# Nineteen adds from GpSimd to VectorE, and written-out tables of buffer places and of instruction orders on all five engines

## The chip, the cores and the metric

One core of a Trainium2 chip runs the kernel. The metric is the device time of one execution in microseconds, lower is better. A core has a matrix engine (TensorE, PE in the profile), three engines that work on tiles (VectorE, DVE; ScalarE, ACT; GpSimd, POOL), a sync engine that here only issues transfers (SyncE, SP), and 16 DMA engines. Each engine works through its own list of instructions in order, and an instruction that has to wait for a semaphore holds up those behind it on its engine.

## The reference

One decoder layer in fp32 with 512 tokens and a model width of 1024. Three token mixers read one normed input, each is gated, and their sum is projected back; a SwiGLU layer follows. Cut to the shape of it:

```python
u = rms_norm(h, ln_mix_pre)
qa, ka, va, qb, kb, vb, qm, gl = split(u @ w_in)
y_swa = sliding_window_attention(qa, ka, va, sinks, rel_bias)   # 8 heads, 2 kv heads, window 128
y_sb  = stick_breaking_attention(qb, kb, vb)                    # 8 heads
y_mem = softmax_attention(qm, rms_norm(mem, ln_mem) @ w_mem_kv) # 4 heads, 256 memory rows
g = sigmoid(gl)                                                 # 3 gates of (512, 1024)
merged = g0 * (y_swa @ w_branch_swa) + g1 * (y_sb @ w_branch_sb) + g2 * (y_mem @ w_branch_mem)
h = h + rms_norm(merged @ w_out, ln_mix_post)
u = rms_norm(h, ln_ffn_pre)
ffn = (silu(u @ w_gate) * (u @ w_up)) @ w_down                  # width 2816
return h + rms_norm(ffn, ln_ffn_post)
```

## The kernel before

**Products.** Each fp32 operand is split into a rounded part (`hi`, or a name that ends in `h`) by a copy on ScalarE (line 137) and the rest (`lo`, or `l`) by a subtraction on VectorE (line 138). A product is three matmuls, lines 169, 170 and 171. The three large products (the gates' part of `w_in`, gate and up, down) are done blockwise with seven products of half-size operands instead of eight, called `p1` to `p7`. Sums of weight blocks that these need are partly formed by the transfers: GpSimd issues a load that adds to a buffer which SyncE's load has filled (line 446 for the gates, 1224 for gate and up, 1364 and 1367 for down).

**Streams.** A `Stream` holds units in the order in which TensorE uses them: a weight tile is loaded some units ahead, split three units ahead, and its matmuls are issued. `dn` is the stream of the token mixers, `fs` that of gate and up. Between the units the program writes the attention work. From this written order, priorities and the dependences, a scheduler at build time makes the list of each engine; pins such as `after(ins, first)` add an order between two instructions without a wait.

**Buffers.** Weight tiles have rings of four (`raw`, `hi`, `lo`); 73 buffers of 128x512 (`ck`) rotate; in PSUM two banks (`psd`) and six (`psa`) rotate apart. For the second half the pools of weights and constants are closed and a new pool of nine raw buffers is opened (`fp`).

**Gates.** `g2p` is the PSUM tile of the third mixer's gate product and `g0p` that of the first's. When a product is complete, `q_end` takes it out: for `p1`, `p5`, `p6` and `p7` by a ScalarE copy (line 540, `gq2p`), which is also what frees the bank for the next product. A branch product `br` (`branch_t`) is multiplied by its gate on VectorE (line 599), and the sum with the other branches is one more add (line 602): GpSimd does it for 14 of the 16 tiles. `merge` transposes the sum, `wo` is the output projection's weight and `mx` its product; `mix` norms it into `mt` (lines 1111 to 1116), `turn` transposes `mt` into `ut`, and `place` (lines 1153 and 1154) writes its split blocks (`B11h` and `B11l` and so on) for the gate and up products `gx`, `gy` and `gw`.

**Down.** `dn_mm` makes the products `x`, `y` and `w` from tiles of `w_down` (`r`, 128x1024, and `bp`, 128x512) and the activations (`aq`, split to `lh` and `ll`). In `p7` the tiles `bp30` to `bp310` of `p3` are used a second time after an adding load.

```python
                g = gate_t[(b, t, h)]
                with tc.high_priority():
                    nc.vector.tensor_tensor(g[:, :], ps[:, :], g[:, :], op=ALU.mult)
                eng = nc.vector if (b, t) == (MEM, NT - 1) else nc.gpsimd
                more = acc_t[(t, h)] if b == SWA else gate_t[(SWA, t, h)]
                eng.tensor_tensor(g[:, :], g[:, :], more[:, :], op=ALU.add)
```

## Time and profile before

| | |
|---|---|
| time, three runs | 787.07, 787.52 and 788.17 us, median 787.52 |
| the profiled execution | 787.54 us, of which the span is 785.7 us |
| granted TensorE clock | 0.999 |
| busy: TensorE / VectorE / ScalarE / GpSimd | 776.3 / 595.4 / 469.3 / 123.2 us |
| the chain that ended last | 93% TensorE, 2% DMA, 2% VectorE, 1% ScalarE |
| moved by DMA | 128.61 MB, mean 164 GB/s |

The span runs from the first instruction to the last; 1.8 us of the profiled time lie around it. Busy is the time in which an engine has an instruction of its own in work. Matmuls are pipelined: a row's duration reaches into the next row, so how fast TensorE goes is read from the distance between two starts.

### The profile page before, as it was taken

To read this page: it belongs to the slowest core of one execution; us is meant where nothing else is said; L and a number is where in the kernel's file an instruction comes from. 1 tells how busy PE (TensorE), PEld (TensorE's weight loads), DVE (VectorE), ACT (ScalarE), POOL (GpSimd) and SP (SyncE) were. 2 spreads that over 40 slices of the span, in tenths; PEclk is the share of its full clock that TensorE was granted. 3 is DMA by queue.
4 is the path that set the end of the run, shared out by engine and by line. 5 is a ranking of instruction groups with operands and counts; after the bars stand their busy time and mean duration, and the time that the engine had idled before them with its cause. 6 is when DMAs were issued, how large, how long until landed. Compare 5 with 4: busy or idle time off the path is not lost.

```text
span 785.7 us, 12335 instructions
## 1 busy us (share of the span) xinstructions
PE 776.3 (99%) x4638; PEld 682.2 (87%) x4638; DVE 595.4 (76%) x942; ACT 469.3 (60%) x837; POOL 123.2 (16%) x142
## 2 busy tenths in 40 slices
PE   9999999999999999999999999999999999999996
PEld 6899887788888888887888899999999999888885
DVE  6995876686877757876855599867677777898797
ACT  7663676686577666657633577455554455666673
POOL 0203400002011111321261000100000000215200
PEclk9999999999999999999999999999999999999999
DMA  8444923265449794369849418987666651949802
GB/s 301 132 138 121 314 88 108 81 190 124 89 100 206 178 208 139 54 170 250 304 162 255 92 47 219 260 220 191 186 180 183 186 155 54 222 107 239 184 1 108
DMA packets 44220, 128.61 MB, mean 164 GB/s; under 512 B 5248, under 2 KB 6832, under 8 KB 44160
## 3 DMA queue, kind: packets, MB, share of 16 engines
q1 hardware_dynamic: 30480, 85.21, 32.8%
q0 software_dynamic: 13248, 42.22, 27.8%
q8 instruction: 36, 0.59, 0.3%
q10 hardware_dynamic: 432, 0.39, 0.1%
q14 instruction: 24, 0.20, 0.1%
HBM read 120.98 MB, written 4.72 MB: 160 GB/s over the span
## 4 chain that ended last, share of the span: by engine, by line
PE 93%; DMA 2%; DVE 2%; issue 1%; ACT 1%; POOL 0%; DVEq 0%; SPq 0%; ACTq 0%; POOLq 0%
PE gx L169 5%; PE gx L171 5%; PE gx L170 5%; PE gy L171 3%; PE gy L169 3%; PE gy L170 3%; PE x L171 3%; PE x L170 3%; PE x L169 3%; PE br L169 2%; PE br L170 2%; PE br L171 2%; PE mx L171 2%; PE mx L170 2%; PE mx L169 2%; PE g1p L169 2%
## 5 line engine op out<-in xcount | busy, mean ns | idle before, releaser
L137 ACT CAST hi<-gw 128x1024 fp32r<-128x1024 f32 x77 | 79.9, 1048 | 92.7 <-DVE gw L1242 39.6
L138 DVE TENSOR_TENSOR lo<-raw,hi 128x1024 fp32r<-128x1024 f32 (+2 forms) x82 | 99.9, 1219 | 46.2 <-ACT hi L137 45.7
L138 DVE TENSOR_TENSOR lo<-gw,hi 128x1024 fp32r<-128x1024 f32 x77 | 93.5, 1223 | 36.2 <-ACT hi L137 36.2
L137 ACT CAST hi<-raw 128x1024 fp32r<-128x1024 f32 (+2 forms) x82 | 85.2, 1042 | 43.4 <-PE pv L171 13.0
L1224 POOL DMA_DIRECT2D gw<-in_w_gu x27 | 23.3, 883 | 196.4 <-DMA gw<-in_w_gu 91.3
L870 DVE TENSOR_TENSOR_SCAN bw<-br,bw 128x512 f32<-128x512 f32 (+3 forms) x32 | 24.4, 808 | 17.0 <-ACT bw L194 17.0
L137 ACT CAST hi<-r 128x1024 fp32r<-128x1024 f32 (+1 forms) x24 | 23.6, 982 | 19.8 <-PE y L171 5.3
L446 POOL DMA_DIRECT2D raw<-in_w_g x24 | 20.7, 862 | 93.2 <-DVE lo L138 74.2
L170 PE MATMUL x<-lo,lh 128*128 128x512 f32 x88 | 34.2, 389 | 0.0
L169 PE MATMUL x<-hi,lh 128*128 128x512 f32 x88 | 34.2, 389 | 0.0
L171 PE MATMUL x<-hi,ll 128*128 128x512 f32 x88 | 34.1, 389 | 0.0
L138 DVE TENSOR_TENSOR lo<-r,hi 128x1024 fp32r<-128x1024 f32 (+1 forms) x24 | 27.1, 1130 | 3.7 <-ACT hi L137 3.6
L137 ACT CAST hi<-bp 128x512 fp32r<-128x512 f32 x33 | 19.3, 620 | 13.4 <-PE y L171 4.8
L138 DVE TENSOR_TENSOR lo<-bp,hi 128x512 fp32r<-128x512 f32 x33 | 22.7, 721 | 6.0 <-ACT hi L137 5.8
L169 PE MATMUL gx<-B11h,hi 128*128 128x256 f32 x88 | 25.1, 285 | 0.2 <-ACT B11h L1153 0.2
L169 PE MATMUL gx<-T4h,hi 128*128 128x256 f32 x88 | 25.0, 285 | 0.0
L169 PE MATMUL gy<-N22h,hi 128*128 128x256 f32 x88 | 25.0, 284 | 0.0
L171 PE MATMUL gy<-N22h,lo 128*128 128x256 f32 x88 | 25.0, 284 | 0.0
L171 PE MATMUL gw<-B21h,lo 128*128 128x256 f32 x88 | 25.0, 284 | 0.0
L170 PE MATMUL gx<-B11l,hi 128*128 128x256 f32 x88 | 25.0, 284 | 0.0
L170 PE MATMUL gw<-B21l,hi 128*128 128x256 f32 x88 | 24.9, 283 | 0.0
L169 PE MATMUL gy<-T1h,hi 128*128 128x256 f32 x88 | 24.9, 283 | 0.0
(824 smaller groups left out, 2758.7 us busy)
## 6 DMA issues: line engine op xcount, KB each, us to landing
gw<-in_w_gu SPq DMA_DIRECT2D x57, 512.0 KB, 4.8
gw<-in_w_gu POOLq DMA_DIRECT2D x27, 512.0 KB, 7.5
raw<-in_w_g POOLq DMA_DIRECT2D x24, 512.0 KB, 6.0
raw<-in_w_g SPq DMA_DIRECT2D x18, 512.0 KB, 3.9
raw<-in_w_p SPq DMA_DIRECT2D x14, 512.0 KB, 4.5
raw<-in_w_brt SPq DMA_DIRECT2D x12, 512.0 KB, 4.8
bp<-in_w_dn SPq DMA_DIRECT2D x22, 256.0 KB, 10.3
r<-in_w_dn POOLq DMA_DIRECT2D x10, 512.0 KB, 9.1
```

Of the source, the lines that this page charges most:

```text
L137: ins = nc.scalar.copy(hi, raw)
L138: lows = nc.vector.tensor_tensor(lo, raw, hi.bitcast(F32), op=ALU.subtract)
L169: one = nc.tensor.matmul(out, lh, rh, start=start, stop=False, skip_group_check=True)
L170: nc.tensor.matmul(out, lh, rl, start=False, stop=False, skip_group_check=True)
L171: return one, nc.tensor.matmul(out, ll, rh, start=False, stop=stop, skip_group_check=True)
L446: nc.gpsimd.dma_start(t[:, :], src, accum_op=ALU.add)
L870: st["scan"] = nc.vector.tensor_tensor_scan(x, r, x, 0.0, op0=ALU.mult, op1=ALU.add)
L1224: nc.gpsimd.dma_start(gw[(n, key)][:, :], g_src(n, i, j), accum_op=ALU.add)
```

## The change

Nineteen tile operations leave GpSimd for VectorE: the 14 gate adds of line 602, three adds of the memory's squares (line 390), one add of 128x256 in `rstd_of` (line 232) and one subtraction of 32x128 (line 810). Six scalings of broadcast gains by -0.5 (line 1058) leave GpSimd for ScalarE. The arithmetic is the same.

Two sets of tables are written out. `PLAN` gives every tile its buffer: four places each for `raw`, `hi` and `lo`, eight PSUM banks `p0` to `p7` that both pools now share, 73 `ck` places, 16 small ones; one pool of weights and constants (`wide0`) stays open through both halves. `ORDER` gives, for each of the five engines, the whole list of its instructions by the number in which the program issues them; `follow` chains each to the one before it, and the pins of `after` fall away. The tables were drawn up with longer transfer times. Smaller edits: the copies `ur` of `turn` are issued later (`kept`), two loads of gate and up move from unit 4 to unit 5, and some tiles are taken when first used (`Late`).

```diff
+ORDER = {
+    "tensor": (
+        "0-17 19 18 20-709 716 719 710-715 717-718 720-754 761 764 755-760 762-763 765-927 940-943 933-936 944 "
...
+    "gpsimd": (
+        "5-12 4 2-3 16 0 29 1 14 13 15 30 17 22 27 21 20 19 18 23 28 25 24 26 31-34 36-37 35 38 40 39 41-49 51 50 "
+        "52-65 70 66 69 71 67-68 72-95 107-112 96-99 103 101 100 102 104-106"
+    ),
...
+PLAN = {
+    "raw": (
+        "0 3 2 1 0 3 2 1 0 3 2 1 0 3 2 1 0 3 2 1 0 3 2 1 0 3 2 1 0 3 2 1 0 3 2 1 0 3 2 3 2 3 2 1 0 1 0 1 0 3 1 2 0 "
...
-    nc = tc.nc
+    nc = Core(tc.nc)
+    places = Places()
...
-    psd = ctx.enter_context(tc.tile_pool(name="psd", bufs=2, space=bass.MemoryType.PSUM))
     psa = ctx.enter_context(tc.tile_pool(name="psa", bufs=6, space=bass.MemoryType.PSUM))
+    psd = psa if PLAN else ctx.enter_context(tc.tile_pool(name="psd", bufs=2, space=bass.MemoryType.PSUM))
...
     def after(ins, first):
+        if not ORDER:
+            follow(ins, first)
+
+    def follow(ins, first):
         dep = mybir.DependencyInfo(mybir.DependencyClass.NoSync, mybir.DependencyReason.DATA)
         tc.add_manual_dep(ins.ins, first.ins.name, dep, reason="order")
...
         if acc.shape[1] > n:
-            nc.gpsimd.tensor_tensor(acc[:, :n], acc[:, :n], acc[:, n : 2 * n], op=ALU.add)
+            nc.vector.tensor_tensor(acc[:, :n], acc[:, :n], acc[:, n : 2 * n], op=ALU.add)
...
             if acc is None:
                 acc = x
             else:
-                nc.gpsimd.tensor_tensor(acc[:, :], acc[:, :], x[:, :], op=ALU.add)
+                nc.vector.tensor_tensor(acc[:, :], acc[:, :], x[:, :], op=ALU.add)
...
-                eng = nc.vector if (b, t) == (MEM, NT - 1) else nc.gpsimd
+                eng = nc.vector
...
-            nc.gpsimd.tensor_scalar(t[h][:, :], t[h][:, :], -0.5, None, op0=ALU.mult)
+            nc.scalar.mul(t[h][:, :], t[h][:, :], -0.5)
...
             for h in range(2):
                 place(("B11", "B21")[h], t, pt[h])
-                nc.scalar.copy(turned[t][h][:, :], pt[h][:, :])
+            st[("kept", t)] = pt
             return
...
-    load_at(4, g_raw, 0, "t", 1, 0)
-    load_at(4, g_plus, 0, "t", 0, 0)
+    load_at(5, g_raw, 0, "t", 1, 0)
+    load_at(5, g_plus, 0, "t", 0, 0)
...
+    for e, text in ORDER.items():
+        seen, last = getattr(nc, e).seen, None
+        for part in text.split():
+            a, _, b = part.partition("-")
+            for k in range(int(a), int(b or a) + 1):
+                if last is not None:
+                    follow(seen[k], seen[last])
+                last = k
```

In the changed kernel every instruction carries line 185, the wrapper's, so its rows are told apart by engine, operation and tile: `p3` is PSUM bank 3, `hi1`, `lo1` and `raw2` are weight places.

ScalarE in the gate products of the third mixer, before. `gq2p50` and `gq2p51` are the copies that free the banks of product `p5`; `hi127` is the rounded part of a weight that an adding load completes:

```order
L194 ACTIVATE gq2p11_3618<-gq2p11_3618,rs_x_299 128x512
L137 CAST hi127_3695<-raw112_3191 128x1024
L540 COPY gq2p50_3706<-g2p50_3671 128x512
L540 COPY gq2p51_3718<-g2p51_3679 128x512
L137 CAST hi128_3720<-raw113_3193 128x1024
L137 CAST wo10h_3737<-wo10_3714 128x512
L137 CAST wo11h_3741<-wo11_3716 128x512
```

The same place after; `hi1_77<-raw2_74` in its last row is the weight of `hi127`:

```order
L185 ACTIVATE gq2p11_3164<-gq2p11_3164,wide0_84 128x512
L185 CAST wo10h_3267<-wo10_3246 128x512
L185 CAST wo11h_3271<-wo11_3248 128x512
L185 COPY gq2p50_3238<-p3_107 128x512
L185 CAST wo02h_3308<-wo02_3290 128x512
L185 COPY gq2p51_3250<-p0_104 128x512
L185 CAST hi1_77<-raw2_74 128x1024
```

The two copies have moved from behind the weight's cast to ahead of it, and three casts of `wo` tiles from behind the copies to ahead of them.

ScalarE some 15 us on, at the end of product `p7`, before; `wo12` and `wo13` are tiles of the output projection that SyncE loads:

```order
L194 ACTIVATE gq2p60_3800<-gq2p60_3800,rs_x_299 128x512
L137 CAST wo12h_3835<-wo12_3809 128x512
L194 ACTIVATE gq2p61_3813<-gq2p61_3813,rs_x_299 128x512
L137 CAST wo13h_3839<-wo13_3811 128x512
L137 CAST hi135_3846<-raw132_3816 128x1024
L540 COPY gq2p70_3856<-g2p10_3586 128x512
L540 COPY gq2p71_3869<-g2p11_3593 128x512
```

The same place after:

```order
L185 ACTIVATE gq2p60_3324<-gq2p60_3324,wide0_84 128x512
L185 ACTIVATE gq2p61_3337<-gq2p61_3337,wide0_84 128x512
L185 COPY gq2p70_3374<-p2_106 128x512
L185 CAST hi0_76<-raw0_72 128x1024
L185 COPY gq2p71_3387<-p4_108 128x512
L185 CAST hi3_79<-raw3_75 128x1024
L185 CAST hi2_78<-raw1_73 128x1024
L185 CAST wo12h_3356<-wo12_3333 128x512
```

The copies of `p7` now follow the two sigmoids at once; `wo12h`, `wo13h` and the cast of `hi135` (now `hi3_79`) stand behind the first of them or both.

TensorE where gate and up begin, before. `gx0` is the first product of gate and up, `gw0` a second one beside it, and `hi151` to `hi153` are the rounded weights of `gx0`, `gw0` and the next product, `gx1`:

```order
L171 MATMUL gx0_4612<-B11h0_3502,lo151_4384 128x256
L169 MATMUL gx0_4612<-B11h1_3504,hi151_4383 128x256
L169 MATMUL gw0_4660<-B21h0_3506,hi152_4493 128x256
L170 MATMUL gw0_4660<-B21l0_3507,hi152_4493 128x256
L170 MATMUL gx0_4612<-B11l1_3505,hi151_4383 128x256
L171 MATMUL gx0_4612<-B11h1_3504,lo151_4384 128x256
```

The same place after. `p2` is `gx0`, `p7` is `gw0`, `p6` is `ut21` (transposes of the normed rows `mt21`), and `p3` is `gx1`, in the bank that held one half of the projected rows (`mx30`) until then:

```order
L185 MATMUL p2_106<-B11h0_3918,lo0_80 128x256
L185 MATMUL p2_106<-B11h1_3922,hi1_77 128x256
L185 MATMUL p7_111<-B21h0_3926,hi3_79 128x256
L185 MATMUL p6_110<-c_ident_329,mt21_3887 128x128 x2
L185 MATMUL p3_107<-B11h0_3918,hi2_78 128x256
L185 MATMUL p3_107<-B11l0_3919,hi2_78 128x256
L185 MATMUL p3_107<-B11h0_3918,lo2_82 128x256
```

The second matmul of `gw0` and the rest of `gx0`'s first half have moved back, and seven matmuls of `gx1` and two transposes have come ahead of them. Just ahead of this piece, the first matmul of `gx0` stood behind the transposes of `ut10` and `ut11` and ahead of the four of `ut20`; it now stands behind three of those four as well.

GpSimd's adding loads of `bp30` to `bp310` in `p7` of down stood in the order 30, 31, 32, 33, 34, 35, 36, 37, 38, 39, 310 and stand now in the order 30, 31, 32, 33, 37, 35, 34, 36, 38, 39, 310. The two scalings of `bc_g_fpost` that stood among them are gone from GpSimd.

More of the change, by code (lines that the diff above doesn't have):

```diff
@@ L1 @@
 import math
[L2 removed]
+from contextlib import ExitStack, nullcontext
 import numpy as np
@@ L147, in w_load @@
         uid[0] += 1
-        raw = wp.tile([P, 1024], F32, tag="raw", name=f"raw{uid[0]}")
+        raw = places.take(wp, "raw", [P, 1024], F32, f"raw{uid[0]}")
         nc.sync.dma_start(raw[:, :n], src)
@@ L215, in tile_kernel @@
     nc.vector.memset(eps_t, EPS)
-    ones = cst.tile([P, P], F32, name="ones")
+    ones = places.fixed(cst, [P, P], F32, "ones")
     nc.vector.memset(ones[:, :], 1.0)
@@ L342, in val @@
         return gen
-    v_all = cst.tile([P, NT * 640], F32, name="v_all")
+    v_all = places.fixed(cst, [P, NT * 640], F32, "v_all")
     def own_values(t):
@@ L730, in first_split @@
         split(raws[i][:, sl], his[i][:, sl], los[i][:, sl])
-    with tc.manual_schedule():
-        idle = cst.tile([P, 512], BF16, name="idle")
+    with nullcontext() if ORDER else tc.manual_schedule():
+        idle = places.fixed(cst, [P, 512], BF16, "idle")
         nc.vector.memset(idle[:, :], 0.0)
@@ L1360, in dn_issue @@
             if p == "p1":
-                rr[c] = fp.tile([P, 1024], F32, tag="raw", name=f"r{c}")
+                rr[c] = places.take(fp, "fraw", [P, 1024], F32, f"r{c}")
                 nc.sync.dma_start(rr[c][:, :n], src)
```

155 lines of the change are left out of this document (125 added, 30 removed), and 91 rows, old and new, of tables (ORDER, PLAN).

## The prediction

> **What bounds the kernel now.** I read the page's busy times first, then the windows of 100 us, then the waits of TensorE, then the chain that ended last around those waits. The page:
>
> ```profile
> PE 776.3 (99%) x4638; PEld 682.2 (87%) x4638; DVE 595.4 (76%) x942; ACT 469.3 (60%) x837; POOL 123.2 (16%) x142
> ```
>
> The windows, with columns span, then busy time and count of TensorE, its weight loads, VectorE, ScalarE and GpSimd, the granted clock and the DMA share:
>
> ```profile
> 0.00:100.00 100.00, 98.64 (x505) 84.12 (x506) 78.74 (x121) 58.58 (x95) 23.11 (x38) 1.00 0.61 199
> ...
> 300.00:400.00 100.00, 98.56 (x480) 82.46 (x480) 71.77 (x102) 59.93 (x106) 25.54 (x22) 1.00 0.59 169
> 400.00:500.00 100.00, 99.83 (x649) 91.07 (x648) 75.93 (x140) 54.07 (x120) 17.59 (x17) 1.00 0.67 177
> 500.00:600.00 100.00, 100.00 (x836) 100.00 (x835) 75.41 (x89) 50.21 (x71) 9.46 (x11) 1.00 0.72 192
> ...
> 700.00:786.00 86.00, 79.29 (x350) 65.31 (x348) 70.86 (x121) 51.27 (x99) 17.71 (x19) 0.99 0.56 132
> ```
>
> TensorE is the bound nearly everywhere, at the full clock. The rows shown lack 1.36 us in the first window, 1.44 in the fourth, 0.17 in the fifth, and the end; they sum to 476.3 of the page's 776.3, so the three left out are full. The waits of TensorE name the same places (engine and line, what it waited for, total, times, longest):
>
> ```profile
> PE g2p L169 <- ACT gq2p L540: 1.4, 2, 1.0
> PE warm L181 <- DVE idle L735: 1.4, 1, 1.4
> PE gx L169 <- ACT B11h L1153: 0.2, 1, 0.2
> ```
>
> The end of TensorE, from the chain (start, duration, what):
>
> ```profile
> 779.07 0.24 PE x L171
> ```
>
> The last matmul is over at 779.31 and the span is 785.7, so 6.4 us follow TensorE: the last norm and the store. Neither this tail nor the start of the first matmuls is touched by the change, and the matmuls are the same in number and shape. What the change can win is therefore what TensorE idles in the middle, 1.6 us by these rows; what it can lose has no such bound.
>
> **The change part by part.** First the two waits for `gq2p`. TensorE around them (start, duration):
>
> ```profile
> 353.88 0.39 PE L171 MATMUL g2p<-hi,xsp51l 128*128 128x512 f32 x1
> 355.02 0.39 PE L170 MATMUL g2p<-lo,xsp51h 128*128 128x512 f32 x1
> 355.24 0.39 PE L171 MATMUL g2p<-hi,xsp51l 128*128 128x512 f32 x1
> 356.60 0.50 PE L169 MATMUL g2p<-hi,xsp30h 128*128 128x512 f32 x1 [0.97 <-ACT gq2p L540]
> 372.82 0.39 PE L171 MATMUL g2p<-hi,ul 128*128 128x512 f32 x1
> 373.68 0.50 PE L169 MATMUL g2p<-hi,uh 128*128 128x512 f32 x1 [0.47 <-ACT gq2p L540]
> ```
>
> Two starts are 0.22 to 0.23 us apart when nothing waits (355.02 to 355.24). At the first wait they are 1.36 us apart, so it costs 1.13; at the second 0.86, so it costs 0.63. Together 1.76 us, a little more than the idle time of the waits view, since the refill of the pipeline counts too. The chain says what held the copies up:
>
> ```profile
> 344.73 10.19 DMA raw<-in_w_g
> 355.01 0.67 ACT hi L137
> 355.97 0.59 ACT gq2p L540
> 365.13 5.29 DMA wo<-in_w_out
> 370.44 0.62 ACT wo12h L137
> 371.60 0.60 ACT wo13h L137
> 372.20 0.96 ACT hi L137
> 373.16 0.48 ACT gq2p L540
> ```
>
> The first copy stood on ScalarE behind a cast whose weight landed at 354.92, though its product was complete at 353.88 + 0.39 = 354.27. In the new order the copy stands ahead of that cast. It then runs from 354.3 to 354.9, and TensorE wants the bank at 355.24 + 0.23 = 355.47: 0.5 us to spare, and the wait is gone. The cast of the weight that was in front is late next; by the rows of the program its first matmul comes after 24 others of the product, some 5.4 us later, against 1.05 for the cast and about 1.2 for VectorE's part, so it stays covered. The second copy of the pair has a `wo` cast of 0.6 us ahead of it and must be done by about 356.8, six matmuls later; its product ends at 355.63, so it ends near 356.3. At the second place the copies now stand ahead of the casts of `wo12` and `wo13`, which waited for a load of 5.29 us. Even by the old times the sigmoids before them are over at 371.6, where `wo13h` began; the product is complete at about 371.85, the copy ends near 372.5, and TensorE wants it at 372.82 + 0.23 = 373.05. Gain: 1.13 + 0.63 = 1.76 us. Both hold as long as ScalarE is not late there by more than half a microsecond; without that cover up to 1.76 us come back.
>
> Next, where gate and up begin. TensorE, ScalarE and VectorE there:
>
> ```profile
> 449.04 1.04 PE L1165 MATMUL ut<-c_ident,mt 128*128 128x128 f32 x8
> 450.25 0.39 PE L169 MATMUL gx<-B11h,hi 128*128 128x256 f32 x1 [0.17 <-ACT B11h L1153]
> 450.53 0.22 ACT L194 ACTIVATE r_m<-t_m 128x1 f32<-128x1 f32 x1
> 451.03 0.21 DVE L1082 SCALAR_TENSOR_TENSOR t_m<-r_m,v_m 128x1 f32<-128x1 f32 x1
> 451.49 0.15 DVE L1083 SCALAR_TENSOR_TENSOR r_m<-t_m,r_m 128x1 f32<-128x1 f32 x1
> 451.89 1.40 DVE L1114 SCALAR_TENSOR_TENSOR mt<-mx,r_m,bc_g_post 128x512 f32<-128x512 f32 x2
> ```
>
> The wait for `B11h` was 0.17 to 0.33 us. Three transposes now stand ahead of it, which hides it. But `gx1` comes forward into the bank that `mt` still reads. Its place is near 451.75: 450.25, then one and seven matmuls of 0.12 (100 us for 836 of them, in the window from 500) and five transposes of 0.11. The `mt` that it waits for can start when `r_m` is there: ScalarE gives its part at 450.75, two small VectorE steps of 0.21 and 0.15 follow, and one `mt` takes half of 1.40, so it ends near 452.0. That is a new wait of 0.25 us for an old one of about 0.3. I count nothing here; the ends are -0.3 and +0.5.
>
> The adds. One GpSimd add, and VectorE beside it:
>
> ```profile
> L602 DVE TENSOR_TENSOR gq2p<-gq2p,gq0p x2: 681/739/797, 391.6 to 404.2; 128x512 f32<-128x512 f32 x2
> 383.06 1.29 POOL L602 TENSOR_TENSOR gq2p<-gq2p,gq0p 128x512 f32<-128x512 f32 x1 [22.22 <-DVE gq2p L599]
> 383.42 1.48 DVE L138 TENSOR_TENSOR wo14l<-wo,wo14h 128x512 fp32r<-128x512 f32 x1 [0.51 <-ACT wo14h L137]
> 384.83 0.68 DVE L138 TENSOR_TENSOR wo15l<-wo,wo15h 128x512 fp32r<-128x512 f32 x1
> ```
>
> On VectorE an add takes 0.74 us (the first row, a median in ns). Seventeen of 128x512 make 12.6 us and the two small ones at most 1. Against that, a VectorE operation that met a GpSimd add took 1.48 where its like took 0.68, so 0.8 us come back for each that meets one: nothing to 14 x 0.8 = 11 us. VectorE's sum grows by 2 to 13 us out of 785, and I take 4. The Trainium skill's "SBUF — State Buffer", section "Who interferes with whom", gives a reason: a VectorE instruction with two SBUF inputs contends with a GpSimd instruction that reads SBUF, and the loser blocks for the whole instruction. By it the second row's 1.29 us less the 0.36 that had passed would be lost, 0.93 against the 0.80 measured, and VectorE's sum would grow by nearly nothing; the trace agrees within 0.15 us. None of it lies on TensorE's path unless VectorE itself runs out of time. The six scalings cost ScalarE about 0.59 each (the `gq2p` copy's row), 3.5 us beside an engine that is 60% busy: nothing.
>
> The transfers. In `p7` of down, the second half of `w_down` tile `bp34` has gone from fifth to seventh of GpSimd's adding loads. ScalarE's casts of these tiles and TensorE's first use:
>
> ```profile
> 733.12 0.62 ACT L137 CAST hi<-bp 128x512 fp32r<-128x512 f32 x1 [1.61 <-PE y L171]
> 736.94 0.62 ACT L137 CAST hi<-bp 128x512 fp32r<-128x512 f32 x1 [1.42 <-PE x L170]
> 738.90 0.62 ACT L137 CAST hi<-bp 128x512 fp32r<-128x512 f32 x1 [1.34 <-DMA bp<-in_w_dn]
> 739.69 0.39 PE L169 MATMUL x<-hi,lh 128*128 128x512 f32 x1
> ```
>
> The tiles come 2 us apart (736.9, 738.9), the fifth at 733.1 and the seventh at 736.9, by the starts of their casts. With cast (0.62) and subtraction (0.68) `bp34` is ready at 738.2, and the matmul that needs its `lo` is the one behind 739.69. The cover shrinks from some 5.5 us to 1.7. I take nothing, with 0 to 3.3 us as the ends (the rival below prices it). The first rows of ScalarE and VectorE and the loads of `w_out` move by about 2 and 10 us against uses that leave more; the start I bound by 0 to 1 us and take 0.2.
>
> The sum, on the profiled execution: 787.54 - 1.13 - 0.63 + 0.2 = 785.8 us, and that execution is 0.02 above the median of the three runs. A measurement of this kernel can tell about 0.2%, 1.6 us, from no change; the forecast is at -0.22%, just outside.
>
> **The rivals.**
>
> *VectorE becomes the bound in the gates (slower).* The windows where it is fullest:
>
> ```profile
> 320.00:330.00 10.00, 10.00 (x57) 8.67 (x56) 9.05 (x18) 6.67 (x19) 3.00 (x4) 1.00 0.30 54
> 330.00:340.00 10.00, 10.00 (x54) 8.49 (x53) 8.60 (x14) 4.93 (x8) 3.50 (x3) 1.00 0.44 94
> ```
>
> It has 20 - 17.65 = 2.35 us free in these 20. The eight adds of the first mixer's gate fall around here; three fit at 0.74 if none gives time back. With all eight and nothing back it is short by 5.9 - 2.35 = 3.6 us, TensorE waits for branch products to be taken out of their banks, and the time is 785.8 + 3.6 = 789.4. For it: the fullest stretch. Against: stretches of 0.8 each come back, and the adds can be spread, since their sums are needed only at the merge. It decides when more than three adds in 20 us give nothing back. The Trainium skill's "Perfetto Trace Analysis", section "Optimizing Scalar/DVE Operations", says that moving work between these two engines might not help, as they share a port; that speaks for a small VectorE sum, not for this rival.
>
> *The adding loads of `w_down` become the bound in `p7` (slower).* If they run 5 us later than before, because the reordered tile at their head waits, 3.3 us of it lies beyond the 1.7 of cover: 785.8 + 3.3 = 789.1. For it: TensorE uses two tiles in 2.7 us (12 matmuls at 0.23), they land in 4, and everything here stands in one fixed order on GpSimd, ScalarE and VectorE. Against: five tiles land ahead of the first use, and the loads of the last gain can now leave this stretch. It decides at 1.7 us.
>
> *The gains are eaten (no change).* TensorE waits nowhere from 500 to 779, so new orders there can only add; a handful of new waits of 0.2 to 0.5 us, with the one at 451.8 and the start, gives back 0.7 to 1.8: 786.5 to 787.6.
>
> *The change does not do what it says (no change).* If ScalarE is late at the two copies for another reason, a load that lands later, both waits stay: 787.5.
>
> **How the numbers follow.** Forecast 0.42; eaten 0.24; not what it says 0.07; VectorE 0.15; `w_down` 0.12. The forecast's own range is 784.8 to 785.9: the waits gone, with 450 at either end and the start at 0 to 0.3. Faster is the forecast, 0.42; no change the next two, 0.31; slower the last two, 0.27. The lower end, 784.7, is all idle of the middle gone (787.54 - 1.76 - 0.33 = 785.5) with 0.8 left for short waits that the views don't list. The upper end, 790.5, takes in both slower cases at their prices and a microsecond more, and leaves out their combination, 785.8 + 6.9.
>
> **What would show it.** Right: in the changed trace no `gq2p` copy ends TensorE's idle time near 355 and 373, the windows from 300 to 400 show TensorE at 99.7 or more of 100, the last matmul ends near 777.6, VectorE's busy time is 597 to 608, and the tail is still 6.4 us. Wrong: a wait of over 0.5 us in TensorE's waits for a `lo` of `bp` in 735 to 750, for VectorE in 320 to 345, or for a transfer anywhere after 500; or a TensorE that starts its second matmul of a pair later than 0.23 us after the first.

## The result, and the profile after

The changed kernel takes 783.96 us (median of six runs, 783.37 to 784.39) where the kernel before, run beside it, takes 787.97 (six runs, 787.07 to 789.26): a ratio of 0.9948, with a 95% interval of 0.9935 to 0.9961. That is 4 us faster, more than twice the forecast gain of 1.7 us, and just under the forecast range. The profiled execution took 784.39 us, the highest of the six; its span is 782.6 us. It is 3.15 us below the profiled execution before (787.54), so the traces below account for some 3 us and not for all of the 4.

The page's busy times, the two windows that had idle time in the middle, and TensorE's waits, of which this is the only row:

```profile
PE 775.0 (99%) x4638; PEld 682.9 (87%) x4638; DVE 601.9 (77%) x961; ACT 472.9 (60%) x843; POOL 88.5 (11%) x117
```

```profile
300.00:400.00 100.00, 100.00 (x490) 84.41 (x489) 78.19 (x121) 58.80 (x106) 6.88 (x8) 1.00 0.59 161
400.00:500.00 100.00, 100.00 (x664) 91.98 (x663) 75.49 (x138) 60.30 (x128) 12.08 (x14) 1.00 0.78 206
```

```profile
PE p L185 <- DVE wide L185: 1.4, 1, 1.4
```

Between its first real matmul and its last TensorE has no wait that the view lists: the windows from 300 to 500 are full. GpSimd lost 35 us, VectorE took up only 6.5 and ScalarE 3.6.

ScalarE and TensorE where the first of the two `gq2p` waits was:

```profile
354.09 0.59 ACT L185 COPY gq2p<-p 128x512 f32<-128x512 f32 x1 [0.72 <-PE p L185]
354.57 0.62 ACT L185 CAST wo02h<-wo 128x512 fp32r<-128x512 f32 x1
355.45 0.59 ACT L185 COPY gq2p<-p 128x512 f32<-128x512 f32 x1 [0.26 <-PE p L185]
355.93 1.05 ACT L185 CAST hi<-raw 128x1024 fp32r<-128x1024 f32 x1
```

```profile
355.02 0.39 PE L185 MATMUL p<-hi,xsp51l 128*128 128x512 f32 x1
355.25 0.39 PE L185 MATMUL p<-hi,xsp30h 128*128 128x512 f32 x1
```

And ScalarE where the second was:

```profile
370.41 0.59 ACT L185 COPY gq2p<-p 128x512 f32<-128x512 f32 x1 [1.31 <-PE p L185]
370.89 1.05 ACT L185 CAST hi<-raw 128x1024 fp32r<-128x1024 f32 x1
371.85 0.58 ACT L185 COPY gq2p<-p 128x512 f32<-128x512 f32 x1
...
374.23 0.62 ACT L185 CAST wo12h<-wo 128x512 fp32r<-128x512 f32 x1
```

Each copy now begins when its own product is done (`<-PE p`), and the weights' casts run behind it; TensorE goes from one product to the next at 0.23 us.

The waits view lists only a few of the places that got shorter. Set side by side, matmul by matmul (4638 in both), the starts of the two traces give this ledger:

| at (time before) | won, us | what stood there before |
|---|---|---|
| start of the program | -0.54 | nothing of the change: TensorE's starts come down from 0.43 to 0.23 us apart later in this execution |
| 131, 140 | 0.23 + 0.21 | `z` waited for ScalarE's copies `at`, whose small piece came last |
| 206 | 0.24 | transposes waited for VectorE's scalings of `w` |
| 355, and the 10 us after it | 1.13 + 0.13 | `gq2p` copy |
| 373 | 0.80 | `gq2p` copy |
| 450 | 0.20 | `B11h`, and what followed |
| 472, 487, 497 | 0.17 + 0.30 + 0.06 | gaps of a tenth or two between gate and up products |
| 300 to 333 | 0.04 | |

That is 3.5 us won and 0.54 lost, 2.96 in all, for the last matmul, whose row in the chain is now this one; it ends at 776.33 by the matmuls themselves, 6.27 us ahead of the span's end:

```profile
769.98 6.36 PE p L185 x28
```

Nothing is lost or won from 500 us on. The gaps in the ledger's row of 472, 487 and 497 look like this in the kernel before: three starts are 0.20 and 0.22 apart, where after the change they are 0.12 apart.

```profile
472.36 0.28 PE L170 MATMUL gy<-T1l,hi 128*128 128x256 f32 x1
472.56 0.39 PE L169 MATMUL gy<-N22h,hi 128*128 128x256 f32 x1
472.78 0.28 PE L170 MATMUL gy<-N22l,hi 128*128 128x256 f32 x1
```

No engine is named there, since TensorE counts as busy through gaps that are shorter than the pipelined end of a matmul.

### The profile page after: what moved, and what is told of

It is laid out like the page before. It is cut to its first block, busy times and chain, and to the rows that moved or that the text cites. A ratio compares the mean times of both kernels' runs of the same rounds, so it can differ in the third digit from the quotient of the medians.

```text
span 782.6 us, 12274 instructions
## 1 busy us (share of the span) xinstructions
PE 775.0 (99%) x4638; PEld 682.9 (87%) x4638; DVE 601.9 (77%) x961; ACT 472.9 (60%) x843; POOL 88.5 (11%) x117
## 4 chain that ended last, share of the span: by engine, by line
PE 99%; DVE 0%; issue 0%; DVEq 0%; ACT 0%
PE p L185 99%; DVE fg L185 0%; DVEq L1893 0%; DVE s L185 0%; DVE wide L185 0%; ACT sqr L185 0%; DVE eps_t L185 0%
## 5 line engine op out<-in xcount | busy, mean ns | idle before, releaser
L185 DVE TENSOR_TENSOR lo<-raw,hi 128x1024 fp32r<-128x1024 f32 (+4 forms) x139 | 159.4, 1154 | 65.5 <-ACT hi L185 64.8
L185 ACT CAST hi<-raw 128x1024 fp32r<-128x1024 f32 (+4 forms) x139 | 137.5, 997 | 96.3 <-PE p L185 60.0
L185 DVE TENSOR_TENSOR lo<-wide,hi 128x1024 fp32r<-128x1024 f32 x53 | 64.8, 1224 | 22.5 <-ACT hi L185 21.9
L185 ACT CAST hi<-wide 128x1024 fp32r<-128x1024 f32 x53 | 55.6, 1052 | 38.6 <-PE p L185 17.8
L185 PE MATMUL p<-lo,lh 128*128 128x512 f32 x154 | 59.9, 389 | 0.0
L185 PE MATMUL p<-hi,ll 128*128 128x512 f32 x154 | 59.7, 389 | 0.0
L185 PE MATMUL p<-hi,lh 128*128 128x512 f32 x154 | 59.3, 389 | 0.0
L185 PE MATMUL p<-lo,uh 128*128 128x512 f32 (+1 forms) x160 | 57.1, 357 | 0.0
L185 PE MATMUL p<-hi,ul 128*128 128x512 f32 (+1 forms) x160 | 57.1, 357 | 0.0
L185 PE MATMUL p<-hi,uh 128*128 128x512 f32 (+1 forms) x160 | 56.9, 358 | 0.0
```

The lines of the kernel that those rows point to most:

```text
L185: ins = f(*args, **kw)
```

## The experiments

All were timed in five rounds beside the kernel before, on one chip for each group, but for the second trace of the kernel before. Theory 1, which I started from, says that the orders of ScalarE and VectorE take single waits away. Rival A gives the adds a cost, rival B says that the tables of places or the loads set the time.

**The adds alone.** The kernel before with the nineteen adds and the six scalings moved, and no tables:

```diff
-                eng = nc.vector if (b, t) == (MEM, NT - 1) else nc.gpsimd
+                eng = nc.vector
...
-            nc.gpsimd.tensor_scalar(t[h][:, :], t[h][:, :], -0.5, None, op0=ALU.mult)
+            nc.scalar.mul(t[h][:, :], t[h][:, :], -0.5)
```

> The kernel before with only the nineteen adds on VectorE and the six scalings on ScalarE, without tables. Theory 1 (the written-out orders of ScalarE and VectorE take TensorE's waits away, and the adds are off its path): no change, ratio 0.999 to 1.001 to the kernel before, both waits of 1.13 and 0.63 us for the gq2p copies still there near 355 and 373, VectorE's busy time near 600. Rival A (the adds: VectorE is no longer stretched by GpSimd and so frees what TensorE waits for sooner): ratio about 0.995, and the two waits gone or under half.

Measured: 787.32 us, ratio 0.9993 (0.9984 to 1.0002). So the adds change nothing in the time that can be told. TensorE's longest wait in that execution, behind the fixed one for the first tile:

```profile
PE g2p L169 <- ACT gq2p L540: 0.9, 1, 0.9
```

There is one `gq2p` wait, at 372, and none at 355, though ScalarE's order there is the old one. The cast that stands ahead of the two copies started sooner, at 353.84 where the kernel before had 355.01:

```profile
353.84 1.05 ACT L137 CAST hi<-raw 128x1024 fp32r<-128x1024 f32 x1 [1.56 <-DMA raw<-in_w_g]
```

So something other than the order makes these waits too, and the adds have a part in it. Set against the trace before, the 1.26 us won at 355 are lost again: 0.6 at 65, where `pv` waits for VectorE's `v_all`, 0.5 at 373 and 0.45 at 743.

**The tables without the gate adds.** The changed kernel with 14 gate adds on GpSimd again:

```diff
-                eng = nc.vector
+                eng = nc.vector if (b, t) == (MEM, NT - 1) else nc.gpsimd
```

> The changed kernel with the fourteen gate adds on GpSimd again, in the place of the order where GpSimd had them; the rest of every engine's order and all places as changed. Theory 1: no change against the changed kernel, ratio to before 0.994 to 0.996, VectorE operations of 0.7 us stretched to 1.5 to 2 beside the adds and TensorE still without a wait. Rival A: half or more of the gain is lost, ratio 0.997 to 1.000.

Measured: 784.07 us, ratio 0.9959 (0.9947 to 0.9972). By the times the tables carry the gain. VectorE was busy 598.7 us against 601.9 with the adds, so 14 adds cost it 3.2 us, not 14 x 0.68 = 9.5. But that TensorE would wait nowhere, as expected, did not hold. Its wait, and ScalarE there:

```profile
PE p L155 <- ACT gq2p L155: 0.9, 1, 0.9
```

```profile
355.59 0.62 ACT L155 CAST wo02h<-wo 128x512 fp32r<-128x512 f32 x1 [1.87 <-DMA wo<-in_w_out]
356.11 0.58 ACT L155 COPY gq2p<-p 128x512 f32<-128x512 f32 x1
```

The new order keeps `wo02h` ahead of the second copy, and here its load is late: TensorE loses 1.10 us from start to start, the first wait of the kernel before again. The adds have a part in it, by way of the loads. This is VectorE's subtraction that frees the buffer for SyncE's next load of w_g, in the kernel before (beside a GpSimd add), in the changed kernel, and in this run:

```profile
340.12 1.29 POOL L602 TENSOR_TENSOR gq0p<-gq0p,bs 128x512 f32<-128x512 f32 x1 [3.90 <-DVE gq0p L599]
340.44 2.06 DVE L138 TENSOR_TENSOR lo<-raw,hi 128x1024 fp32r<-128x1024 f32 x1 [0.40 <-ACT hi L137]
```

```profile
340.22 1.23 DVE L185 TENSOR_TENSOR lo<-raw,hi 128x1024 fp32r<-128x1024 f32 x1 [0.40 <-ACT hi L185]
```

```profile
339.26 2.06 DVE L155 TENSOR_TENSOR lo<-raw,hi 128x1024 fp32r<-128x1024 f32 x1 [0.40 <-ACT hi L155]
```

Beside an add on GpSimd it takes 2.06 us instead of 1.23. SyncE's load, and the six of w_out behind it, go out that much later, and the last of the six then come behind GpSimd's adding load: in the kernel before the sixth is issued at 345.27 and the adding load at 344.73, in this run the fifth (`wo02`) at 343.61 and the adding load at 343.54; in the changed kernel all six are out by 344.21, ahead of the adding load at 344.50. The one issued behind landed late, at 355.08 and 355.51; in the changed kernel the last of the six landed at 350.48. So in these traces TensorE waits at 355 with the adds on GpSimd under the old order and under the new one, and with the adds on VectorE under neither. The times don't resolve that: 0.9959 and 0.9948 have intervals that overlap.

**The places without the orders.** The changed kernel with an empty table of orders:

```diff
-ORDER = {
...
+ORDER = {}
```

> The changed kernel with the table of orders emptied, so that the scheduler draws up the order again; the adds stay on VectorE and the table of places stays. Theory 1: the gq2p copies fall back behind the casts and the waits near 355 and 373 are back, ratio 0.999 to 1.002. Rival B (the places: eight PSUM banks shared by both pools let TensorE go on without waiting): ratio about 0.995 and no wait for the copies. Rival A: 0.995 as well.

Measured: 807.05 us, ratio 1.0242 (1.022 to 1.0263), far from what was expected. TensorE's longest waits:

```profile
PE p L110 <- ACT gq1p L110: 8.5, 3, 7.1
PE p L110 <- ACT gq2p L110: 3.7, 1, 3.7
```

The places are no gain by themselves: under an order that they were not drawn up for they come with waits of 7 and 4 us. The reverse, the orders with the old places, was not tried.

**Some of the old order back.** The changed kernel with ScalarE's order of before at the two `gq2p` places and the eight triples of `at`, and VectorE's at 206 us; in the table of ScalarE, at one of these places:

```diff
-386-387 383 390 384 382 391 385 388-389
+382-391
```

> The changed kernel with the order undone at five kinds of place and nothing else: on ScalarE the two gq2p places and the three copies of each attention turn (at, largest first again), on VectorE the recip and scalings of one softmax near 206 behind a weight's subtraction. Theory 1: the waits come back one by one, 1.13 at 355, 0.6 to 0.8 at 373, 0.2 each at 131 and 140, 0.25 at 206, together 2.4 us: 786.4 us, ratio 0.998. Rivals A and B: nothing comes back, ratio 0.995.

Measured: 793.92 us, ratio 1.0086 (1.0073 to 1.01). TensorE's waits:

```profile
PE p L133 <- DVE lo L133: 3.3, 1, 3.3
PE p L133 <- ACT gq2p L133: 2.0, 1, 2.0
```

The loss is 10 us where some 2.4 had been expected: ScalarE's old order beside VectorE's new one makes waits that neither kernel has, such as 3.3 us for a `lo`. This undid too much at once to tell the price of one place.

**Two copies mended in the kernel before.** Here theory 1 is put to the test alone: pins put the `gq2p` copies ahead of the cast that stood in front of them at 355 and 373.

```diff
+    for late, copy in ((382, 384), (400, 402)):
+        after(seen[late], seen[copy])
```

> The kernel before, with one thing changed: on ScalarE the copies of the gate pieces that TensorE waits for at 355 and 373 us (`gq2p`) stand ahead of one 128x1024 cast each, as in the changed kernel. Tables of places, adds and all other orders are as before. Theory 1 (the written-out orders of ScalarE and VectorE take single waits away, and nothing pays them back): 1.13 and 0.80 us less, ratio 0.9976, within 0.997 to 0.9985 (some executions of the kernel before lack the first wait, so less than the whole may show). Rival B (the tables of places, not the orders, brought the gain, or a wait that goes comes back later): 0.9995 to 1.001, with a new wait of TensorE somewhere between 355 and 500 us.

Measured: 787.92 us, ratio 1.0001 (0.9992 to 1.001). Theory 1 falls. The wait at 355 is gone, but the waits view has three others, and ScalarE shows why:

```profile
PE g2p L199 <- ACT gq2p L118: 1.2, 3, 0.7
```

```profile
363.21 1.05 ACT L118 CAST hi<-raw 128x1024 fp32r<-128x1024 f32 x1 [0.89 <-DMA raw<-in_w_g]
...
365.68 1.05 ACT L118 CAST hi<-raw 128x1024 fp32r<-128x1024 f32 x1 [0.89 <-DMA raw<-in_w_g]
...
367.15 1.06 ACT L118 COPY gq2p<-g2p 128x512 f32<-128x512 f32 x2
```

The loads of w_g come in one each 2.5 us (365.68 - 363.21), and the next copies stand behind the next cast that waits for one. TensorE's starts lose 0.85, 0.31 and 0.56 us at 367, 373 and 375: 1.72, where the two waits before made 1.76. The time won at 355 only let TensorE run sooner into the next load. (The profiled execution, 789.29 us, is one of the longest of the twelve: its matmuls began 0.61 us later than the trace before, and lost 1.1 us at 743 in a wait for `lh` that neither the trace before nor that of the next run has.)

**Four places.** The two copies, and the two other orders of the ledger, `at` and the scalings at 206 us:

```diff
+        nc.scalar.copy(at[2][:, :384], pt[2][:, :384])
         nc.scalar.copy(at[0][:, :], pt[0][:, :])
...
+    after(nc.vector.seen[266], nc.vector.seen[262])
```

> As the run with the two copies, and two more orders as in the changed kernel: of ScalarE's three copies of the turned weights (`at`), the small third piece goes first at all eight heads (0.23 and 0.21 us at 131 and 140 us), and VectorE's four scalings by 1/sum at 206 us stand ahead of one 128x1024 remainder (0.24 us). Theory 1: 2.6 us less than before, ratio 0.9967, within 0.996 to 0.9975, that is 0.5 to 0.7 us below the two copies alone. Rival B: no lower than the two copies alone.

Measured: 787.18 us, ratio 0.9996 (0.9988 to 1.0005). Its median is 0.74 us below that of the two copies; the intervals overlap, but the trace agrees, where 0.5 us is won on the kernel before from 131 to 210 us and kept to the end (the ledger has 0.68 for these places). These small waits are won for good: no later one gives them back. The `gq2p` waits are those of the run before.

**The row of copies.** Theory 2, formed on that: a copy behind a cast waits for that cast's load, and only a row that is in order from end to end is rid of it. With two more pins the gate copies from 350 to 376 us stand ahead of the weights' casts that held them up, as in the changed kernel. `wo12h` and `wo13h` were left where they stood.

```diff
-    for late, copy in ((382, 384), (400, 402)):
+    for late, copy in ((382, 384), (392, 394), (395, 401), (400, 402)):
```

> The kernel before with the four places, and two more: the gate copies (`gq2p`) of 365 to 366 us stand ahead of the cast of the next 128x1024 load, and the one of 373 us ahead of the cast after it. So of the changed kernel's ScalarE order from 350 to 376 us only the place of `wo12h` and `wo13h` is missing. In the run with the four places TensorE waited 0.78, 0.32 and 0.59 us from 365 to 374, behind casts whose loads landed 2.4 to 2.5 us apart. Theory 2 (a copy that stands behind a cast waits for that cast's load; a single place that is mended hands the wait to the next one, a whole row that is mended doesn't): the 0.78 and most of the rest go, 1.0 to 1.4 us less than the four places, ratio 0.998 (0.997 to 0.9987). Rival B (the loads pace TensorE there whatever the order, and the tables of places changed the loads): the wait comes back between 366 and 380, no lower than the four places, 0.9995.

Measured: 787.19 us, ratio 0.9993 (0.9984 to 1.0002), no lower than the four places. The wait at 365 is gone, and again it stands one place on, now behind the very two casts that were left:

```profile
PE g2p L200 <- ACT gq2p L118: 1.9, 2, 1.5
```

```profile
370.86 0.62 ACT L118 CAST wo12h<-wo 128x512 fp32r<-128x512 f32 x1 [2.73 <-DMA wo<-in_w_out]
...
...
372.52 0.57 ACT L118 COPY gq2p<-g2p 128x512 f32<-128x512 f32 x1
```

**The row, without those loads.** The same kernel, with the loads of `wo12` and `wo13` left out:

```diff
+        if (h, q) == (1, 1):
+            st[("wo", h, q)] = list(st["wo last"])
+            return
```

> The kernel before with the row of copies (six places of the orders), and the two 256 KB loads of w_out left out that are issued at 364 us (`wo12`, `wo13`; the tiles of the two loads before are used in their place, so the output isn't the reference's). In the run with the row of copies, ScalarE stood 2.73 us at 368 to 371 for the first of them, with a gate copy behind its cast, and TensorE waited 1.70 us for that copy and 0.56 us for the next. Theory 2 (each wait is a copy behind a cast that waits for its load; with the last such cast out of the way there is none left): both go, 1.7 to 2.3 us less than the row of copies, ratio 0.997 (0.9963 to 0.9979), and no wait over 0.3 us from 350 to 440. Rival B (a wait that goes comes back elsewhere, since the loads or VectorE pace that stretch): 0.9985 to 1.000, with a new wait between 366 and 385.

Measured: 786.09 us, ratio 0.9979 (0.997 to 0.9988), 1.1 us below the row of copies by the medians. The waits of TensorE, and ScalarE at the same place:

```profile
PE warm L212 <- DVE idle L118: 1.4, 1, 1.4
PE ss_x L212 <- DVE xacc L118: 0.3, 1, 0.3
PE gx L200 <- ACT B11h L118: 0.2, 1, 0.2
```

```profile
368.29 0.62 ACT L118 CAST wo12h<-wo 128x512 fp32r<-128x512 f32 x1
...
370.62 0.59 ACT L118 COPY gq2p<-g2p 128x512 f32<-128x512 f32 x1 [0.58 <-PE g2p L202]
```

No `gq2p` wait is left in the list (starts show one of 0.22 us at 373), and none has come up behind. That agrees with theory 2: with no late load ahead of a copy the stretch runs free. Since two loads are gone as well, it doesn't rule out by itself that the loads are the bound; the late casts put back, below, try the same place with every load there. The ratio came out at the upper end of what was expected, 0.9979.

**Four loads less.** The test from the other side: the order as it was, the loads earlier. Four 256 KB loads of w_out ahead of those of w_g are left out.

```diff
+        if (h, q) in ((1, 0), (0, 1)):
+            st[("wo", h, q)] = list(st["wo first"])
+            return
```

> The kernel before, with four of the six 256 KB loads of w_out left out that are issued from 343 to 345 us (the first two tiles are used in their place, so the output isn't the reference's). All orders but one cast's are as before. The loads of w_g share the DMA engines with them: from 345 us on they would land up to 4 x 256 KB / 214 GB/s = 4.9 us earlier. Theory 2: TensorE's waits at 355 (1.13 us) and 373 (0.63 us) go with ScalarE's order as it was, 1.5 to 2 us less, ratio 0.998 (0.9972 to 0.9985). Rival B: the orders alone make the waits, and they stay, 0.9995 to 1.0005.

Measured: 786.98 us, ratio 0.9992 (0.9984 to 1.0001). One of the two waits goes, that at 355, and that at 371 stays:

```profile
PE g2p L169 <- ACT gq2p L540: 0.5, 1, 0.5
```

That is less than half of what was expected: the second wait hangs on `wo12`, as in the row of copies, and its load was not among the four. GpSimd's adding load, issued at 344.50, landed at 350.82 here, 6.3 us after its issue where the kernel before has 10.2. So the first wait needs both, a copy behind the cast and a load that is late; take either away and it goes.

**One copy back in the changed kernel.** The cast of 356 us ahead of the two copies again:

```diff
-386-387 383 390 384 382 391 385
+386-387 382-383 390 384 391 385
```

> The changed kernel with one thing put back: on ScalarE the 128x1024 cast of 356 us stands again ahead of the two gate copies of 354 and 355.5 us. That cast's load landed at 352.92 us or at 356.02 us, depending on which of two it is. Theory 2: TensorE waits there for 0.9 to 1.5 us, and as the places behind are in order nothing is given back: 1 us more than the changed kernel, 0.996 to 0.9968 of before. If the load is the earlier of the two there is no wait, and the time is the changed kernel's (0.995); that would speak for the loads. Rival B: the changed kernel's time, wait or not, since the loads behind get that much more time.

Measured: 783.52 us (five runs, 783.4 to 783.85), ratio 0.9948 (0.9935 to 0.9961): the changed kernel's time. No wait came:

```profile
352.31 1.05 ACT L162 CAST hi<-raw 128x1024 fp32r<-128x1024 f32 x1
353.27 0.57 ACT L162 COPY gq2p<-p 128x512 f32<-128x512 f32 x1
```

Of the two cases in the expectation it was the one with the earlier load: the cast found its weight there at 352.31, without an idle time in front. In the changed kernel this load lands at 352.9, in the kernel before at 354.92. SyncE's six loads of w_out, which hold it up (the run with four loads less), are issued a microsecond sooner than before; SyncE's rows of before and after:

```profile
342.94 2.75 SPq L1067 DMA_DIRECT2D wo<-in_w_out  x6
```

```profile
341.85 2.79 SPq L185 DMA_DIRECT2D wo<-in_w_out  x6
```

So at 355 either of two things takes the wait away: both copies ahead of every cast that waits for a load, as in the run with the two copies, or loads that land in time, as here and in the run of the adds alone. The changed kernel has the second, by its adds. Its order moved the copies ahead of one such cast but left the second behind another, `wo02h`, and alone it did not take the wait away (the tables without the gate adds).

**The late casts back in the changed kernel.** `wo12h` and `wo13h` ahead of the copy of 370.4 us again, in the table of ScalarE:

```diff
-392 396 399 401 395 402 400 403 397
+392 396 399 397-398 401 395 402 400 403
```

> The changed kernel with one thing put back: on ScalarE the casts of `wo12h` and `wo13h` stand ahead of the gate copy of 370.4 us, as before the change. Their loads landed at 370.35 and 370.97 us. Theory 2: the copy is held to 371.5 us, TensorE waits 0.9 to 1.4 us for it, and the casts of the loads behind it are late too, so nothing is given back: 0.9 to 1.5 us more than the changed kernel, ratio to before 0.9961 to 0.9968. Rival B: no wait or one that is given back, 0.9948 to 0.9954.

Measured: 784.36 us (five runs, 784.03 to 784.95), ratio 0.9963 (0.995 to 0.9975). By the medians that is 0.4 us over the changed kernel and 0.8 over the run with one copy back, timed in other groups; the wait itself is plain in the trace:

```profile
PE p L162 <- ACT gq2p L162: 0.5, 1, 0.5
```

```profile
370.06 0.62 ACT L162 CAST wo12h<-wo 128x512 fp32r<-128x512 f32 x1 [1.28 <-DMA wo<-in_w_out]
...
371.27 0.58 ACT L162 COPY gq2p<-p 128x512 f32<-128x512 f32 x1
```

It costs TensorE 0.65 us from start to start, less than the 0.9 expected: the copy ended at 371.27 + 0.58 = 371.85 and TensorE could have used its bank at 371.26, so the expectation's hold was right and its figure for the wait too long. Nothing gave the wait back. With the row without late loads, this is the same place from both sides, and here every load is there.

**More work on VectorE.** The changed kernel with one more 128x512 operation on VectorE behind each of the 16 gate adds, and with three more:

```diff
+                for _ in range(1):
+                    nc.vector.tensor_tensor(g[:, :], g[:, :], g[:, :], op=ALU.max)
```

> The changed kernel, with one more VectorE operation of 128x512 (a maximum of the gate piece with itself, 0.68 us) behind each of the 16 gate adds: 8 of them from 317 to 341 us, where VectorE is busy 18.5 of 20 us, and 8 from 383 to 402. Theory 1 (VectorE has room behind the ring of gate pieces; TensorE doesn't wait for it): up to 1 us more, ratio to the changed kernel up to 1.0013, thus 0.995 to 0.9965 of before. Rival A (VectorE is the bound from 320 to 340 once its free time is gone): 5.5 us of new work less 1.5 to 2.4 us free, so 3 to 4 us more than the changed kernel, 0.9985 to 1.000 of before, with TensorE waiting for VectorE there.

> The changed kernel with three more such VectorE operations behind each of the 16 gate adds: 16.4 us of new work from 317 to 341 us and 16.4 us from 383 to 402. Theory 1: the room behind the ring is some 8 to 12 us (VectorE is busy 55 to 80% of the 60 us that follow), so 4 to 8 us more than the changed kernel. Rival A: all that the free time doesn't hold stands on TensorE's path, 16.4 less 2 us from 317 to 341 and 10 us or so from 383 to 402, so 14 to 25 us more than the changed kernel.

Measured: with one more 783.88 us, ratio 0.9954 (0.9941 to 0.9967), nothing lost; with three more 805.61 us, ratio 1.0229 (1.0214 to 1.0243). The windows from 320 to 340 with one more, and from 320 to 330 with three more:

```profile
320.00:330.00 10.00, 10.00 (x54) 8.32 (x53) 9.70 (x25) 5.98 (x18) 0.86 (x1) 1.00 0.33 55
330.00:340.00 10.00, 10.00 (x54) 8.48 (x53) 9.90 (x15) 5.34 (x8) 0.86 (x1) 1.00 0.32 52
```

```profile
320.00:330.00 10.00, 5.69 (x35) 4.74 (x34) 9.76 (x17) 1.76 (x9) 0.86 (x1) 0.94 0.34 53
```

VectorE is a bound here, but further off than the rival had it: 5.5 us of new work (8 x 0.68) fill it to 19.60 of 20 us, and TensorE doesn't notice. Three times that stops TensorE for 4.3 us in one piece, and more behind it. The loss of 21.7 us is within what rival A expected, above what theory 1 did.

**The kernel before once more.**

> The kernel before once more, for a second trace of it. Its runs lie between 786.5 and 789.3 us, 2.8 us apart, those of the changed kernel within 1.0 us. Theory 2: the 2.8 us are waits for gate copies behind casts, whose sum changes with the time at which the loads land: from 350 to 380 us other waits than 1.13 and 0.63 us, at other places, and about the same outside of it. Rival: the difference lies at the start of the program (the time at which the full clock is granted).

Measured: 787.89 us, one run. Its waits:

```profile
PE g2p L169 <- ACT gq2p L540: 1.8, 2, 1.1
PE kb L181 <- ACT uh L247: 0.6, 1, 0.6
```

The two `gq2p` waits are at the same places as in the first trace, and 0.34 us longer from start to start (1.27 and 0.83); the start of the program is 0.06 us later. With the run of the adds alone, which lacks the first wait, that is a spread of one microsecond in these waits, of the 2.8 us between the lowest and the highest run of the kernel before. The start of the program, the rival, spreads as far: TensorE's 21st matmul begins between 7.74 and 8.77 us in the traces of these sixteen runs, and later starts are moved by the same amount. Which of the two made a given run long was not found.

## Why the prediction was right or wrong

**The sign was right, and the mechanism in part.** The waits at 355 and 373 went, windows from 300 to 400 are full, VectorE's 601.9 us lie in the 597 to 608 named, 450 gave no new wait over 0.5 us, and nothing was lost from 500 on. The last matmul ends at 776.33 instead of near 777.6, and the tail is 6.27 us where 6.4 was named.

**The step that failed is the ceiling: "What the change can win is therefore what TensorE idles in the middle, 1.6 us by these rows".** The rows were those of the windows and of the waits view, and both miss gaps under the pipelined end of a matmul. The windows that the prediction took for full, 100 to 300, lost 0.68 us. Counted from start to start the ledger has another 0.23 + 0.21 + 0.24 + 0.53 us at 131, 140, 206 and 472 to 497. The lower end of the range allowed 0.8 for "short waits that the views don't list" and needed 1.2. This is a term that was left out, and the trace of before had it: the starts could have been listed.

**Terms that were mis-sized.** The sum itself, 787.54 - 1.13 - 0.63 + 0.2, is 785.98; the 785.8 on record lacks the 0.2. 355 was 1.13, as summed, and 0.13 more in the closer spacing behind it. 373 was 0.80, where 0.63 was summed: the matmuls behind the wait are a little slower too. 450 was 0.20, where nothing was counted, within its ends of -0.3 and +0.5: the new wait for `mt` didn't come. The start, 0.2 in the sum, is no term of the change: it differs by up to a microsecond from trace to trace.

**The reason for the two gains was wrong at 355 and incomplete at 373.** The prediction has the copies move ahead of the cast, and the wait at 355 go by the order; of the adds it says "None of it lies on TensorE's path unless VectorE itself runs out of time". The traces show another path: a GpSimd add makes a VectorE subtraction 0.83 us longer (2.06 against 1.23), which holds up SyncE's loads, and the late load holds up the cast ahead of the copy. With the adds on VectorE the load of 354.92 lands at 352.92 in the changed kernel, and the wait is gone even under the old order (the adds alone, one copy back); with the new order and the gate adds on GpSimd it is back, behind `wo02h`. The runs that show this have one trace each, the kernel before has two. The prediction's own condition, that a ScalarE half a microsecond late brings the wait back, named the risk. At 373 the order is what counts: with the late casts back, ScalarE waits 1.28 us for a load and TensorE loses 0.65. But one pair of it is not enough: in the kernel before, moving the copies at 355 and 373 brings 0.0 us (ratio 1.0001), because the next copy stands behind the next load. That the two gains came out near their sum is luck in so far as the first had another cause.

**The rivals.** VectorE as the bound of 320 to 340 did not come, and its point of decision, more than three adds in 20 us, was too low: eight more in 24 us cost nothing, 24 more cost much. That the adds would cost VectorE little held (3.2 us for 14; 3.1 for all nineteen in the run of the adds alone, where 4 were taken): the row that showed a VectorE operation of 1.48 us beside a GpSimd add pointed the right way. The Trainium skill's "SBUF — State Buffer", section "Who interferes with whom", has a VectorE instruction with two SBUF inputs contend with a GpSimd instruction that reads SBUF; the 2.06 us beside an add agree. The adding loads of `w_down` made no wait. The gains were not eaten: the new orders added no wait after 500. That ScalarE is late at the copies for a load did not come in the changed kernel's trace, but it did at 355 with the adds back on GpSimd.

**What the parts come to.** Adds alone 0.9993, tables without the gate adds 0.9959, both 0.9948: by the times the tables are the gain, and the adds, alone or on top, can't be told from nothing. By the traces the adds take away the wait at 355, 1.1 to 1.3 us of the 3.5 in the ledger. Of the rest, experiments reproduced in the kernel before 0.5 of the 0.7 us of `at` and the scalings (by trace; by medians 0.74, with intervals that overlap), and 1.5 of the 2.1 us of both `gq2p` waits (row without late loads, by trace, and with two loads less). The 0.7 us from 450 to 497 were not tried alone: what made them is read from the two traces only.

## What to carry to other kernels

List the starts of the bound engine, matmul by matmul, before naming a ceiling for a change: small gaps that no waits view lists made a third of this gain. On an engine with one queue, a wait is not one pair of instructions but a row: ahead of what frees the bound engine's buffers, count every instruction that waits for a load, for mending the first hands the wait to the second. When work sits on an engine off the bound's path, ask whose operations it stretches and which transfers wait for those: here an add at 340 us helped decide when a load landed 15 us later. And a table of places is worth only what its order is worth: test them together, or expect a loss.

## What the runs showed of the hardware that was not expected

After a long stop TensorE ran at about half speed for a while. In the run with some of the old order back:

```profile
365.87 0.80 PE L133 MATMUL p<-lo,xsp60h 128*128 128x512 f32 x1 [3.35 <-DVE lo L133]
366.46 0.63 PE L133 MATMUL p<-hi,xsp60l 128*128 128x512 f32 x1
366.89 0.63 PE L133 MATMUL p<-hi,xsp60h 128*128 128x512 f32 x1
```

The starts from 366.46 to 371.57 are 0.43 us apart, 12 times, where 0.23 is normal and with the first matmul's 0.59 the stop of 3.35 us costs 2.8 us more. The granted clock of these 10 us was 0.67:

```profile
365.00:375.00 10.00, 9.13 (x29) 7.31 (x30) 5.86 (x7) 2.12 (x3) 1.72 (x2) 0.67 0.74 147
```

The same came after stops of 2.0, 3.2, 3.7, 4.3 and 7.1 us in these runs, for eight matmuls or more, and after none up to 1.7 us; one stop of 2.2 us (for a `wo` cast, in the run with three more operations each) passed without it. So this wait cost nearly twice its length, and those of one microsecond that this case is about cost their length and some tenths. The Trainium skill's "TensorE: Matmul & The Clock Gate", section "Part 1: The HAM clock gate (the "warmup" mystery)", says that the clock is halved after an idle window of about 3.4 us and that the windows run on freely. The half rate agrees with the 0.43 us here; that stops as short as 2.0 us set it off, and one of 2.2 us did not, agrees with the free windows but not with a window that must be idle from end to end. The same page has the slow matmuls at the start of a kernel vary with the windows from run to run; the spread of a microsecond at the start, 7.74 to 8.77 us for the 21st matmul, agrees with that.

VectorE, too, had more room than its busy time told: 19.60 of 20 us without a wait of TensorE.
